# The second matrix of the last feed-forward network: seven block products in place of eight, in a half-pair order

## The chip, the cores and the metric

The kernel runs on one NeuronCore of a Trainium2 chip. The metric is the device time of one execution in microseconds (us). TensorE (PE) multiplies, VectorE (DVE) and ScalarE (ACT) do the elementwise work, GpSimd (POOL) does a little of it and issues some transfers, SyncE (SP) issues the loads of the weights. Each engine takes its instructions in the order in which they stand in its own queue.

## The reference, cut to what matters

A two-layer decoder trunk on 256 tokens of width 1024 in float32. Each layer is a mixer between two feed-forward networks; a last normalisation follows.

```python
def swiglu(h, w_in, w_out):            # w_in [1024, 5632], w_out [2816, 1024]
    gate, up = jnp.split(h @ w_in, 2, axis=-1)
    return (jax.nn.silu(gate) * up) @ w_out

for i in range(2):
    x = x + 0.5 * swiglu(rms_norm(x, ffn_norm[i, 0]), ffn_w_in[i, 0], ffn_w_out[i, 0])
    x = x + mixer(rms_norm(x, mix_norm[i]))     # 0: gMLP, 1: stick-breaking attention
    x = x + 0.5 * swiglu(rms_norm(x, ffn_norm[i, 1]), ffn_w_in[i, 1], ffn_w_out[i, 1])
return rms_norm(x, final_norm)
```

The change concerns the last `swiglu` (i = 1, second network) and the normalisation behind it.

## The kernel before, in words

Every matrix product is made of three TensorE products: each operand is split exactly into two float32r parts, `hi` (a cast on ACT) and `lo` (source minus hi, on DVE), and `mm3` adds lo·hi, hi·lo and hi·hi.

The weights are one stream of pieces of 128 x 1024 numbers (512 KB), in the order of use, kept by the class `Weights`. `run_to` (L66 to L88) issues a load on SP and, later, the split of a piece: an ACT cast (L81) and a DVE subtraction (L83). `get` asks for loads `RAW_AHEAD` = 7 and splits `SPLIT_AHEAD` = 5 pieces ahead of the piece in use; there are 7 buffers for raw pieces and 9 each for hi and lo.

A feed-forward network goes through 11 pairs of blocks ("pairs", 256 hidden features each). `ffn_in` multiplies the pair's gate and up columns (four pieces, 96 TensorE products of 256 columns) into two PSUM banks; DVE scales them by 1/rms (L449, L451), ACT applies silu (L450), DVE multiplies (L452), and the result is split (L153, L154). Two pairs later the pair's two pieces of the second matrix are multiplied. In the last network this is `out_add`: stationary the hidden block (128 features x 128 tokens), moving 512 columns of the weights, into four banks; 2 feature halves x 2 token halves x 2 column halves x 3 = 24 products of 512 columns for each pair, so eight block products for each pair.

At the start of the last network `norm.columns` and `norm.rows` (tag `pstf`) turn the sum of squares `acc`, which POOL adds up (L288), into 1/rms (`rT`, `diag`, `rb`). `back` transposes the residual stream and ACT copies it to `xo` (L812). Behind the last pair the output is finished in pieces of 512 and 256 columns: DVE adds (L854), ACT squares, DVE and ACT scale (L868, L870), SP stores (L873).

The order in an engine's queue is set by the framework's scheduler, which may take an instruction ahead of another that it deems late. `tc.keep_in_program_order` puts an instruction behind whatever was traced last for its engine. The stick-breaking attention ahead of the last network has its order written out by hand (`ATT_STEPS`).

Of the kernel before, what the change touches and what calls it, by code (L numbers as in the profile page):

```python
# [38 lines left out]
class Weights:  # L39
    """The weight matrices as a stream of [128, 1024] pieces in the order of use. Each is loaded  # L40
    once and split exactly into two float32r parts, w = hi + lo, some pieces ahead of its use."""

    def __init__(self, tc, raw_pool, hi_pool, lo_pool):
        self.nc = tc.nc
        self.keep_order = tc.keep_in_program_order
        self.strict = False
        self.behind = 0  # so many pieces keep their place
        self.piece = UNIT
        self.pools = raw_pool, hi_pool, lo_pool
        self.sources = []  # L50
        self.raw = {}
        self.parts = {}
        self.loaded = 0
        self.split = 0
# [36 lines left out]
    def get(self, i, inner):  # L91
        self.run_to(i + 1 + RAW_AHEAD, i + 1 + min(SPLIT_AHEAD, 2 + i // 2))
        hi, lo = self.parts.pop(i)
# [6 lines left out]
def trunk(  # L100
# [29 lines left out]
    hp = ctx.enter_context(tc.tile_pool(name="hp", bufs=4))  # L130
    scr = ctx.enter_context(tc.tile_pool(name="scr", bufs=8))
    small = ctx.enter_context(tc.tile_pool(name="small", bufs=3))
    pg = ctx.enter_context(tc.tile_pool(name="pg", bufs=4, space=PSUM))
    py = ctx.enter_context(tc.tile_pool(name="py", bufs=4, space=PSUM))

    def gbank(name):
        return pg.tile([P, 512], F32, tag="pg", name=name)

    def ybank(name):
        return py.tile([P, 512], F32, tag="py", name=name)  # L140

    def scratch(name, width=512):
        return scr.tile([P, width], F32, tag="scr", name=name, padded_shape=[P, 516])

    def mm3(o, a, b, first, last):
        """o (+)= a.T @ b for a, b each given as two float32r parts."""
# [9 lines left out]
    # The gMLP's blocks of 256 features: the u products, the mixing behind them, the products into  # L156
    # the residual stream behind that.
# [44 lines left out]
    plan11 = plan_ffn(1, 1)  # L202

# [39 lines left out]
    def warm_up(n):  # L243
        """Products of nothing, that wake the tensor engine's clock while the first loads run."""
# [24 lines left out]
    def prepare(d, gains, sq=True):  # L269
        """The parts of x*g of chunk d for the next products, and its share of the mean square."""  # L270
# [22 lines left out]
    def newton(o, root, v, w):  # L293
        """o = v**-0.5 from an estimate of v**0.5, with a step of Newton's; w is scratch."""
# [34 lines left out]
    def load_x(hf):  # L329
        """Half of x into the residual stream, its parts and its squares."""  # L330
# [33 lines left out]
    def bc2(ap):  # L364
        """[128, n] -> [128, 2, n], the same twice."""
# [6 lines left out]
    class Residual:  # L372
        """y.T = sum over chunks of W[chunk].T @ h[chunk], in four banks."""
# [50 lines left out]
    def project_rows(o, ids, xs, mid={}):  # L424
        """x.T W for a block of 256 features: [tokens, features] of two halves."""
# [17 lines left out]
    def ffn_in(tag, j, ids, mid={}, by_bank=False):  # L443
        """silu(gate) * up of 256 features, in two parts."""
# [16 lines left out]
    def ffn(tag, plan, gains, mid={}, by_bank=False, extra={}):  # L461
        """extra: what else is done ahead of a block's products into the residual stream."""
# [15 lines left out]
    # ======== layer 0: gMLP ========  # L478
# [17 lines left out]
    def spatial_weights(hf):  # L496
        """The causal W_s, transposed, and what the LayerNorm's shift and b_s add behind it:
        b_c * (row sum of W_s)[t] + b_s[t]."""
        gg = slice(hf * 4, hf * 4 + 4)
        nc.gpsimd.affine_select(  # L500
            ws3[:, gg],
            ws3[:, gg],
            pattern=[[0, 4], [-1, P]],
            compare_op=ALU.is_ge,
            fill=0.0,
            base=0,
            channel_multiplier=1,
# [394 lines left out]
```

## Time and profile before

| what | value |
|---|---|
| time, median of 3 runs | 1018.98 us (1018.62 to 1019.21) |
| profiled execution: its own time from first to last instruction (span) | 1016.9 us |
| TensorE busy | 998.7 us (98%), 8044 products |
| VectorE busy | 651.4 us (64%) |
| ScalarE busy | 499.6 us (49%) |
| GpSimd busy | 84.0 us (8%) |
| mean granted TensorE clock | 0.998 of full speed |
| DMA | 177 GB/s on the mean |

The profile gives no time for the profiled execution beyond its span; the median of the runs is 2.1 us above that span. Products of TensorE are pipelined, so one of them "takes" longer than the distance to the next; what counts is the distance between starts.

### The profile page before, as it was taken

Reading aid. Unit: us, or ns where it says so; the run is one execution under the profiler, and the core shown is the slowest. Engines: PE = TensorE matmul, PEld = TensorE weight load, DVE = VectorE, ACT = ScalarE, POOL = GpSimd, SP = SyncE. Lnnn points to the kernel's source line nnn. Section 1 sums busy time; section 2 is a strip of 40 time slices with the busy share of each in tenths; the row PEclk is TensorE's granted clock in tenths of the full one; section 3 lists DMA queues with packets and bytes.
Section 4 is the critical chain, followed back from the end, with each engine's and each line's share of the span. In section 5 each row is a group of like instructions: output and inputs, shape, how many; then the busy total and the mean of one; then the engine's idle time right before and its main releaser. Section 6 shows DMA issues by size and latency. Waiting matters only on the chain.

```text
span 1016.9 us, 19320 instructions
## 1 busy us (share of the span) xinstructions
PE 998.7 (98%) x8044; PEld 979.4 (96%) x8044; DVE 651.4 (64%) x852; ACT 499.6 (49%) x683; POOL 84.0 (8%) x122
## 2 busy tenths in 40 slices
PE   9999999999999999999999999999998899999997
PEld 8999999999999999999999999999998799999996
DVE  6865665676766774646569655564679975655553
ACT  7543434475544553434348444443476565444433
POOL 3000000010000300000003000000036420000002
PEclk9999999999999999999999999999999999999999
DMA  9965555656545365655564756555642436656511
GB/s 310 325 187 174 185 179 176 187 161 212 186 167 167 125 214 183 187 184 187 180 190 141 239 185 187 182 188 181 193 132 65 137 117 219 188 185 191 183 42 42
DMA packets 135208, 179.56 MB, mean 177 GB/s; under 512 B 5624, under 2 KB 119376, under 8 KB 135120
## 3 DMA queue, kind: packets, MB, share of 16 engines
q1 hardware_dynamic: 134768, 177.76, 54.9%
q8 instruction: 63, 1.03, 0.4%
q0 software_dynamic: 192, 0.52, 0.2%
q14 instruction: 25, 0.20, 0.1%
q10 hardware_dynamic: 160, 0.05, 0.0%
HBM read 176.73 MB, written 1.05 MB: 175 GB/s over the span
## 4 chain that ended last, share of the span: by engine, by line
PE 88%; DVE 6%; issue 2%; ACT 1%; DMA 1%; POOL 1%; SPq 0%; ACTq 0%; POOLq 0%; DVEq 0%
PE yo L148 2%; PE yo L150 2%; PE yo L149 2%; PE gb L148 2%; PE uc L149 2%; PE gc L148 2%; PE ub L149 2%; PE yb L148 2%; PE uc L150 2%; PE ub L150 2%; PE ub L148 2%; PE gb L150 2%; PE uc L148 2%; PE ud L150 2%; PE gc L150 2%
## 5 line engine op out<-in xcount | busy, mean ns | idle before, releaser
L81 ACT CAST whi<-raw 128x1024 fp32r<-128x1024 f32 (+1 forms) x333 | 342.3, 1044 | 403.3 <-issue 219.2
L83 DVE TENSOR_TENSOR wlo<-raw,whi 128x1024 fp32r<-128x1024 f32 (+1 forms) x333 | 400.9, 1221 | 203.2 <-ACT whi L81 202.4
L288 POOL TENSOR_TENSOR acc<-acc,sq 128x256 f32<-128x256 f32 x39 | 33.9, 870 | 566.9 <-ACT sq L287 564.9
L148 PE MATMUL ga<-xnh,wlo 128*128 128x256 f32 x176 | 50.7, 288 | 0.0
L148 PE MATMUL ya<-hha,wlo 128*128 128x256 f32 x176 | 50.0, 284 | 0.1
L148 PE MATMUL yc<-hhc,wlo 128*128 128x256 f32 x176 | 50.0, 284 | 0.1
L148 PE MATMUL yb<-hhb,wlo 128*128 128x256 f32 x176 | 50.0, 284 | 0.0
L148 PE MATMUL gd<-xnh,wlo 128*128 128x256 f32 x176 | 50.0, 284 | 0.0
L148 PE MATMUL gb<-xnh,wlo 128*128 128x256 f32 x176 | 49.9, 283 | 0.0
L148 PE MATMUL gc<-xnh,wlo 128*128 128x256 f32 x176 | 49.9, 283 | 0.0
L149 PE MATMUL ya<-hla,whi 128*128 128x256 f32 x176 | 49.8, 283 | 0.0
L149 PE MATMUL yb<-hlb,whi 128*128 128x256 f32 x176 | 49.8, 283 | 0.0
L149 PE MATMUL yc<-hlc,whi 128*128 128x256 f32 x176 | 49.7, 283 | 0.0
L150 PE MATMUL ud<-xnh,whi 128*128 128x256 f32 x176 | 49.7, 282 | 0.0
L150 PE MATMUL uc<-xnh,whi 128*128 128x256 f32 x176 | 49.6, 282 | 0.0
L149 PE MATMUL ub<-xnl,whi 128*128 128x256 f32 x176 | 49.6, 282 | 0.0
L149 PE MATMUL uc<-xnl,whi 128*128 128x256 f32 x176 | 49.6, 282 | 0.0
L150 PE MATMUL yb<-hhb,whi 128*128 128x256 f32 x176 | 49.6, 283 | 0.0
L148 PE MATMUL ua<-xnh,wlo 128*128 128x256 f32 x176 | 49.6, 282 | 0.0
L150 PE MATMUL ga<-xnh,whi 128*128 128x256 f32 x176 | 49.6, 282 | 0.0
L150 PE MATMUL ub<-xnh,whi 128*128 128x256 f32 x176 | 49.6, 282 | 0.0
L149 PE MATMUL gd<-xnl,whi 128*128 128x256 f32 x176 | 49.5, 281 | 0.0
(286 smaller groups left out, 3367.1 us busy)
## 6 DMA issues: line engine op xcount, KB each, us to landing
raw<-in_ffn_w_in_dram SPq DMA_DIRECT2D x176, 512.0 KB, 4.6
raw<-in_ffn_w_out_dram SPq DMA_DIRECT2D x88, 512.0 KB, 4.2
raw<-in_a_w_in_dram SPq DMA_DIRECT2D x32, 512.0 KB, 4.4
raw<-in_a_w_out_dram SPq DMA_DIRECT2D x16, 512.0 KB, 3.3
raw<-in_b_w_q_dram SPq DMA_DIRECT2D x8, 512.0 KB, 4.4
raw<-in_b_w_o_dram SPq DMA_DIRECT2D x8, 512.0 KB, 4.3
raw<-in_w_kv_dram SPq DMA_DIRECT2D x4, 512.0 KB, 4.2
xin<-in_x_dram SPq DMA_DIRECT2D x4, 256.0 KB, 4.5
```

The lines of the kernel that those rows point to most:

```text
L81: ins = nc.scalar.copy(hi[:, cc], raw[:, cc])
L83: ins = nc.vector.tensor_sub(lo[:, cc], raw[:, cc], hi[:, cc].bitcast(F32))
L148: nc.tensor.matmul(o, al, bh, start=first, stop=False, skip_group_check=True)
L149: nc.tensor.matmul(o, ah, bl, start=False, stop=False, skip_group_check=True)
L150: nc.tensor.matmul(o, ah, bh, start=False, stop=last, skip_group_check=True)
L288: nc.gpsimd.tensor_add(acc, acc, s)
```

## The change

In the last network the second matrix is multiplied by a scheme with seven block products for ten of the eleven pairs. For a pair, A is the hidden block as 2 x 2 blocks (token half by feature half) and B the 256 x 1024 weights as 2 x 2 blocks of 128 x 512. The eight products A·B become seven products of sums of blocks, each into a PSUM bank of its own (`q[1]` to `q[7]`) that is kept through all ten pairs; the four output blocks are put together from the seven banks at the end. The eleventh pair is multiplied plainly (`plain`).

What goes with it:

- The sums of A (`sums`: four DVE operations of 128 columns) are made in float32 from the hidden block, which is kept in the free halves of `xT`; then seven of the eight blocks are split (`parts`: an ACT cast and a DVE subtraction of 896 columns).
- The sums of B are made by accumulating transfers that POOL issues. `load` brings three blocks by SP; `first` splits these three (1536 columns) and issues one accumulating transfer of 512 KB; `second`, one half-pair later, splits two sums (1024 columns) and issues two accumulating transfers of 256 KB, the second of which reads what the first writes; `third`, a pair later, splits two more sums (1024 columns).
- The first matrix is multiplied by half pairs (`in_half`: gate and up of 128 features, 48 products) into one bank, `pi`, which has a single buffer from pair 2 on (the second halves of pairs 0 and 1 use another).
- From the last network's first normalisation on, all ACT, DVE, POOL and SP work is pinned to the order of the program; each pair's four pieces of the first matrix are split during the pair before (`weights`).
- For room in SBUF the whole kernel's stream has `RAW_AHEAD` 5, `SPLIT_AHEAD` 4, 5 raw buffers and 7 each for hi and lo.
- The final sums, squares and scalings are written anew for the seven banks (`finish`). One `affine_select` of the gMLP is pinned.

The core of the diff (comments are dropped in the new file):

```diff
-RAW_AHEAD = 7
-SPLIT_AHEAD = 5
+RAW_AHEAD = 5
+SPLIT_AHEAD = 4
...
-    rawp = ctx.enter_context(tc.tile_pool(name="rawp", bufs=7))
-    hip = ctx.enter_context(tc.tile_pool(name="hip", bufs=9))
-    lop = ctx.enter_context(tc.tile_pool(name="lop", bufs=9))
+    rawp = ctx.enter_context(tc.tile_pool(name="rawp", bufs=5))
+    hip = ctx.enter_context(tc.tile_pool(name="hip", bufs=7))
+    lop = ctx.enter_context(tc.tile_pool(name="lop", bufs=7))
...
+    psum.close()
+    pi = ctx.enter_context(tc.tile_pool(name="pi", bufs=1, space=PSUM))
+    pools["y"] = ctx.enter_context(tc.tile_pool(name="pq", bufs=7, space=PSUM))
...
+    pin = tc.keep_in_program_order
+
+    def pinned_split(h, l, src):
+        pin(nc.scalar.copy(h, src))
+        pin(nc.vector.tensor_sub(l, src, h.bitcast(F32)))
...
+        def load(self, j):
+            t = fm.tile([P, 3, 512], F32, tag="raw", bufs=3, name=f"fraw{j}")
+            for s, (m, n) in enumerate(((1, 1), (0, 0), (1, 0))):
+                pin(nc.sync.dma_start(t[:, s, :], self.block(j, m, n)))
...
+        def first(self, j):
+            p = self.parts[j] = {}
+            p["B22"], p["B11"], p["B21"] = self.split(j, 0, 0, 3)
+            pin(
+                nc.gpsimd.dma_start(
+                    self.raw[j][:, 0:2, :],
+                    self.block(j, 0, 1).unsqueeze(1).broadcast_to([P, 2, 512]),
+                    accum_op=ALU.add,
+                )
+            )
+
+        def second(self, j):
+            p = self.parts[j]
+            p["R3"], p["R1"] = self.split(j, 1, 0, 2)
+            t = self.raw[j]
+            pin(nc.gpsimd.dma_start(t[:, 1, :], self.block(j, 1, 1), accum_op=ALU.add))
+            pin(nc.gpsimd.dma_start(t[:, 2, :], t[:, 1, :], accum_op=ALU.add))
+
+        def third(self, j):
+            p = self.parts[j]
+            p["R2"], p["R4"] = self.split(j, 2, 1, 3)
...
+    PRODUCTS = {
+        1: ("A11", "B11"),
+        2: ("A12", "B21"),
+        3: ("S4", "B22"),
+        4: ("A22", "R4"),
+        5: ("S1", "R1"),
+        6: ("S2", "R2"),
+        7: ("S3", "R3"),
+    }
+    UNITS = NPAIR - 1
...
+    def weights(p):
+
+        W.run_to(first_id + p + 1 + RAW_AHEAD, first_id + p + 1)
...
+    def gate_up(j, m, bank):
+        gu = gus[j, m] = scratch(f"gud{j}_{m}")
+        pin(nc.vector.tensor_mul(pair(gu), pair(bank), bc2(rb)))
+        pin(nc.scalar.activation(gu[:, :T], gu[:, :T], AF.Silu))
+
+    def hidden(j, m):
+        f = fs[j] = xT[:, (j % 2) * 4 : (j % 2) * 4 + 4, :].rearrange("p a (b t) -> p (a b) t", b=2)
+        gu = gus.pop((j, m))
+        pin(nc.vector.tensor_mul(f[:, 2 * m : 2 * m + 2, :], pair(gu[:, :T]), pair(gu[:, T:])))
+
+    def sums(j):
+        f = fs[j]
+        pin(nc.vector.tensor_sub(f[:, 4, :], f[:, 2, :], f[:, 0, :]))
+        pin(nc.vector.tensor_sub(f[:, 6, :], f[:, 0, :], f[:, 1, :]))
+        pin(nc.vector.tensor_add(f[:, 5, :], f[:, 4, :], f[:, 1, :]))
+        pin(nc.vector.tensor_sub(f[:, 7, :], f[:, 3, :], f[:, 5, :]))
...
+    def rows():
+        norm.rows()
+        back()
+        W.strict = True
+
+    for j in range(NPAIR):
+        last = j == NPAIR - 1
         for m in range(2):
...
+            if m == 0 and j < UNITS:
+                forms.load(j)
+            in_half(j, m, bank, (norm.columns, rows) if (j, m) == (0, 0) else ())
+            if m == 0:
+                weights(4 * j + 4)
+                if j:
+                    parts(j - 1)
+                if j > 1:
+                    forms.third(j - 2)
+                weights(4 * j + 5)
+                gate_up(j, m, bank)
+                if 0 < j:
+                    forms.second(j - 1)
+                hidden(j, m)
+                if j == 2:
+                    q = {n: ybank(f"q{n}") for n in range(1, 8)}
+                if j > 1:
+                    out_add(j - 2, (1, 2, 3, 5))
+            else:
+                weights(4 * j + 6)
+                if not last:
+                    forms.first(j)
+                gate_up(j, m, bank)
+                weights(4 * j + 7)
+                hidden(j, m)
+                if not last:
+                    sums(j)
+                if j > 1:
+                    out_add(j - 2, (7, 6, 4))
+    parts(NPAIR - 1)
+    forms.third(UNITS - 1)
...
+    out_add(UNITS - 1, (1, 5, 7))
...
+    out_add(UNITS - 1, (6,))
...
+    out_add(UNITS - 1, (2, 3, 4))
...
+    plain(2, ("A11", "A12"), 0)
...
+    plain(3, ("A11", "A12"), 1)
...
+    plain(8, ("A21", "A22"), 1)
+    finish(1, 2)
...
+    for i in range(2):
+        cc = slice(i * 256, (i + 1) * 256)
+        plain(4, ("A21", "A22"), 0, cc)
+        add(xo[:, 0, cc], q[4][:, cc], 0.5, xo[:, 0, cc])
+        square(0, 1 + i, cc)
+    finish(0, 3)
```

## Rows read from the trace of the kernel before

**Rows 1.** Engines' busy time in two stretches: attention, and one pair.

```profile
757.00:805.00 48.00, 40.45 (x282) 36.11 (x282) 47.09 (x76) 31.76 (x65) 30.62 (x54) 1.00 0.38 119
...
863.50:880.30 16.80, 16.80 (x121) 15.82 (x120) 9.53 (x11) 7.11 (x9) 0.00 (x0) 1.00 0.59 186
```

**Rows 2.** Waits: engine and line, what it waited for, total, times, longest.

```profile
DVE gsd L449 <- PE gd L150: 30.2, 10, 10.8
```

**Rows 3.** TensorE in order of time at the borders of blocks of the last network.

```profile
846.38 0.48 PE L148 MATMUL yo<-whi,hld 128*128 128x512 f32 x1
...
981.23 0.40 PE L148 MATMUL yo<-whi,hld 128*128 128x512 f32 x1
...
986.72 0.28 PE L148 MATMUL gd<-xnh,wlo 128*128 128x256 f32 x1
...
998.08 0.40 PE L148 MATMUL yo<-whi,hld 128*128 128x512 f32 x1
...
1009.26 0.28 PE L150 MATMUL yo<-whi,hhd 128*128 128x256 f32 x1
```

**Rows 4.** Groups by line and shape in the last network: busy us, mean ns.

```profile
L83 DVE TENSOR_TENSOR wlo<-raw,whi 128x1024 fp32r<-128x1024 f32 x59 | 71.0, 1220 | 41.5 <-ACT whi L81 41.4
L81 ACT CAST whi<-raw 128x1024 fp32r<-128x1024 f32 x59 | 60.9, 1047 | 81.3 <-issue 45.0 <-PE gd L150 34.3 <-PE yo L150 1.7
...
L449 DVE TENSOR_TENSOR gsd<-gd,rb 128x512 f32<-128x512 f32 x11 | 7.6, 691 | 30.2 <-PE gd L150 30.2
...
L452 DVE TENSOR_TENSOR usd<-usd,gsd 128x512 f32<-128x512 f32 x11 | 7.5, 686 | 0.1
L450 ACT ACTIVATE gsd<-gsd 128x512 f32<-128x512 f32 x11 | 6.9, 628 | 12.8 <-DVE gsd L449 12.8
```

**Rows 5.** VectorE, then ScalarE, in order of time, where instructions follow without a wait.

```profile
897.81 1.21 DVE L83 TENSOR_TENSOR wlo<-raw,whi 128x1024 fp32r<-128x1024 f32 x1
898.94 0.68 DVE L452 TENSOR_TENSOR usd<-usd,gsd 128x512 f32<-128x512 f32 x1
899.54 1.21 DVE L83 TENSOR_TENSOR wlo<-raw,whi 128x1024 fp32r<-128x1024 f32 x1
...
897.49 0.63 ACT L450 ACTIVATE gsd<-gsd 128x512 f32<-128x512 f32 x1
898.02 1.04 ACT L81 CAST whi<-raw 128x1024 fp32r<-128x1024 f32 x1
```

**Rows 6.** From sum of squares to rb, four engines; then the copies to xo.

```profile
820.13 5.98 POOL L288 TENSOR_TENSOR acc<-acc,sq 128x256 f32<-128x256 f32 x7 [16.97 <-ACT sq L287]
...
826.81 0.50 PE L311 MATMUL pstf<-ones,acc 128*128 128x1 f32 x4
...
828.66 0.26 ACT L316 ACTIVATE rootf<-pstf,eps 128x2 f32<-128x2 f32 x1
...
828.95 0.16 DVE L317 TENSOR_SCALAR varf<-pstf 128x2 f32<-128x2 f32 x1 [3.44 <-ACT rootf L316]
...
829.81 0.48 DVE L320 TENSOR_SCALAR diag<-ident,rT 128x128 f32<-128x128 f32 x2
...
834.33 0.36 ACT L325 COPY rb<-pstf 128x256 f32<-128x256 f32 x1
...
845.73 2.02 ACT L812 COPY xo<-xb 128x512 f32<-128x512 f32 x4
```

**Rows 7.** Transfers: queue, count, KB each, median us from issue to landing.

```profile
raw<-in_ffn_w_out_dram SPq DMA_DIRECT2D x88, 512.0 KB, 4.2
...
out_dram<-xo SPq DMA_DIRECT2D x4, 256.0 KB, 2.0
...
kzh<-kzh POOLq DMA_DIRECT2D x2, 128.0 KB, 6.2
```

**Rows 8.** Behind the last product: VectorE, then ScalarE.

```profile
1009.77 0.42 DVE L854 SCALAR_TENSOR_TENSOR xo<-yo,xo 128x256 f32<-128x256 f32 x1
...
1012.57 0.91 ACT L870 ACTIVATE xo<-xo,fr 128x256 f32<-128x256 f32 x2 [0.93 <-DVE fr L298]
```

More of the change, by code (lines that the diff above doesn't have):

```diff
@@ L201, in trunk @@
     plan_o = [W.add(rows(b_w_o[0], P * b)) for b in range(8)]
-    plan11 = plan_ffn(1, 1)
+    plan11 = [
+        [[W.add(cols(ffn_w_in[1, 1], c0 + 256 * j, kh)) for c0 in (0, DFF)] for kh in range(2)] for j in range(NPAIR)
+    ]
+    plan_d = [W.add(rows(ffn_w_out[1, 1], 256 * (NPAIR - 1) + P * m)) for m in range(2)]
     xin = {}
@@ L499, in spatial_weights @@
         gg = slice(hf * 4, hf * 4 + 4)
[L500 to L507, printed above, removed]
+        tc.keep_in_program_order(
+            nc.gpsimd.affine_select(
+                ws3[:, gg],
+                ws3[:, gg],
+                pattern=[[0, 4], [-1, P]],
+                compare_op=ALU.is_ge,
+                fill=0.0,
+                base=0,
+                channel_multiplier=1,
+            )
         )
@@ new lines, in in_half @@
+    def in_half(j, m, bank, mid=()):
+        for kh in range(2):
+            if m == 0:
+                wd[kh] = [W.get_split(i, 256) for i in plan11[j][kh]]
+            for k4 in range(4):
+                k = kh * 4 + k4
+                for n, w in enumerate(wd[kh]):
+                    mm3(
+                        bank[:, n * T : (n + 1) * T],
+                        tuple(t[:, k4, m * P : (m + 1) * P] for t in w),
+                        (xnh[:, k, :], xnl[:, k, :]),
+                        k == 0 and n == 0,
+                        k == KC - 1,
+                    )
+            if kh < len(mid):
+                mid[kh]()
@@ L804, in back, with parts @@
+    def parts(j):
+        s0, s1 = (1, 8) if j < UNITS else (0, 4)
+        h = fm.tile([P, s1 - s0, P], F32R, tag="fsh", name=f"fsh{j}", padded_shape=[P, 7, P])
+        l = fm.tile([P, s1 - s0, P], F32R, tag="fsl", name=f"fsl{j}", padded_shape=[P, 7, P])
+        pinned_split(h, l, fs.pop(j)[:, s0:s1, :])
+        fparts[j] = {n: (h[:, s - s0, :], l[:, s - s0, :]) for n, s in SLOT.items() if s0 <= s < s1}
     def back():
@@ L811, in back @@
                     )
-                nc.scalar.copy(xo[:, tt, hf * 512 : (hf + 1) * 512], bank)
-    norm = Rms("f3")
-    hs = {0: ffn_in("d", 0, plan11["in", 0], {1: norm.columns, 2: norm.rows}), 1: ffn_in("d", 1, plan11["in", 1])}
-    back()
-    banks = [ybank(f"yo{i}") for i in range(4)]
-    def out_add(w, h, first, last, tts):
-        for tt in tts:
-            for hf in range(2):
-                mm3(
-                    banks[tt * 2 + hf],
-                    tuple(t[:, tt * P : (tt + 1) * P] for t in h),
-                    tuple(t[:, hf * 512 : (hf + 1) * 512] for t in w),
-                    first,
-                    last,
-                )
@@ new lines, in trunk, with at, add @@
+    parts(NPAIR - 1)
+    forms.third(UNITS - 1)
+    tail = [W.get_split(i, UNIT) for i in plan_d]
+    q[8] = pi.tile([P, 512], F32, tag="pi", name="q8")
+    gf = rawp.tile([P, D], F32, tag="raw", name="gf")
+    nc.sync.dma_start(gf, final_norm.unsqueeze(0).broadcast_to([P, D]))
+    def at(tt, n):
+        return xo[:, tt, n * 512 : (n + 1) * 512]
+    def add(o, a, scale, b, op=ALU.add):
+        nc.vector.scalar_tensor_tensor(o, a, scale, b, ALU.mult, op)
+    ss = {tt: small.tile([P, 4], F32, tag="ss", name=f"ss{tt}") for tt in range(2)}
@@ L864, in trunk @@
-        newton(r[:, 0:1], root, v[:, 2:3], r[:, 1:2])
-        for i, cc in enumerate(pieces):
-            o = xo[:, tt, cc]
-            if i == 1:
-                nc.vector.tensor_scalar_mul(o, o, r[:, 0:1])
-            else:
-                nc.scalar.mul(o, o, r[:, 0:1])
-        for hf in range(2):
-            cc = slice(hf * 512, (hf + 1) * 512)
-            nc.sync.dma_start(out[tt * P : (tt + 1) * P, cc], xo[:, tt, cc])
+        nc.vector.reduce_sum(v, ss[tt][:, :n], axis=mybir.AxisListType.X)
@@ new lines, in finish, with plain @@
+        nc.vector.tensor_scalar(v, v, 1.0 / D, RMS_EPS, ALU.mult, ALU.add)
+        nc.scalar.activation(root, v, AF.Sqrt)
+        newton(r[:, 0:1], root, v, r[:, 1:2])
+        nc.vector.tensor_scalar_mul(at(tt, 0), at(tt, 0), r[:, 0:1])
+        nc.scalar.mul(at(tt, 1), at(tt, 1), r[:, 0:1])
+        for h in range(2):
+            nc.sync.dma_start(out[tt * P : (tt + 1) * P, h * 512 : (h + 1) * 512], at(tt, h))
+    def plain(n, a, half, cc=slice(0, 512)):
+        for m in range(2):
+            c0 = half * 512
+            mm3(
+                q[n][:, cc],
+                fparts[NPAIR - 1][a[m]],
+                tuple(t[:, c0 + cc.start : c0 + cc.stop] for t in tail[m]),
+                n == 8 and m == 0,
+                m == 1,
+            )
```

117 lines of the change are left out of this document (77 added, 40 removed).

## The prediction

> **What bounds the kernel now.** I read the busy times first: TensorE is busy in practically all of a pair's 16.8 us, VectorE in 9.5 [rows 1]. Then the waits: VectorE's scaling of the gate waits for TensorE, 30 us in the last network, while TensorE waits for nobody there [rows 2]. So a product removed from TensorE is worth its full distance as long as the others keep up, and the reader should look at how much room they have.
>
> The order of TensorE's work gives the prices [rows 3]. From 981.23 to 986.72 stand 24 products of 512 columns, 0.229 us each; from there to 998.08 stand 96 of 256 columns, 11.36 us, with the change of block in it. A pair takes 16.85 us.
>
> **What is removed.** Ten pairs lose three products of 512 columns each: 10 x 3 x 0.229 = 6.9 us. A pair becomes 11.36 + 21 x 0.229 = 16.17 us, some 16.2 with the second change of block that the half-pair order brings.
>
> **What is added for VectorE and ScalarE.** From the groups, a VectorE operation of 1024 columns lasts 1.22 us and one of 512 lasts 0.69, an ACT cast of 1024 lasts 1.05 and a silu of 512 lasts 0.63 [rows 4]. Without a wait the next VectorE operation starts 1.13 us behind one of 1024 and 0.60 behind one of 512, and ACT's next 0.53 behind a silu of 512 [rows 5]. Scaled along these lines: 128 columns occupy VectorE 0.20 us, 256 0.33, 896 1.00, 1536 1.66; a silu of 256 holds ACT 0.32. A hop from engine to engine I put at 0.04 (828.66 + 0.26 to 828.95 is 0.03) [rows 6].
>
> All of this is pinned, so I follow the queue. Behind the gate of a second half VectorE needs: scaling 0.69, silu 0.32 (cast may follow), cast of a piece 1.05, hops 0.1, in all 2.15 us in which it has nothing else, since the subtraction of that piece stands next; then the subtraction 1.13, `hidden` 0.42, the four sums 0.96 (two wait for the one before), a subtraction 1.13, `parts` 1.00, `third` 1.13, a subtraction 1.13. That is 9.05 us from gate to gate. Behind the gate of a first half: 2.15 again, `second` 1.13, `hidden` 0.33, a subtraction 1.13, `first` 1.66, that is 6.40. Sum 15.45 us against TensorE's 16.2. In the steady state TensorE still sets the pace, with 0.75 us to spare; the single bank `pi` costs nothing there, because 12 and 9 products stand between two halves.
>
> **The start of the last network** has no such cover: pairs 0 and 1 have no products of the second matrix, 11.4 us of TensorE work each, against VectorE's loop. And the loop starts late. The sum of squares is complete at 820.13 + 5.98 = 826.11; column products 0.5, root 0.26, scale to `diag` 1.34 (828.95 to 830.29), row products about 0.5 as well, `rb` 0.36, with the hops 829.3 [rows 6]. Behind `rb` ACT's pinned queue holds the four copies to `xo`, 2.0 us in before [rows 6], which today come when nobody needs ACT; then the cast of piece 4. Subtractions of pieces 4 and 5, then: first gate of pair 0 at 834.8. I continue with the loop: without `second`, `first` waits for its own cast (1.47 us behind that of piece 6), so the second gate comes 5.2 us later, at 840.0; pair 1 at 847.9 (9.05 without `third`) and 854.3; pair 2 at 863.35. Only then is `pi` free, and the second half of pair 2 (5.68 us) ends at 869.75.
>
> TensorE alone would be there at 846.38 (today's start of the first second-matrix block, the same work behind it) + 5.68 + 12 x 0.229 + 5.68 = 860.5 [rows 3]. So 9.2 us are lost, first to pieces 7 and 11, which are split behind a gate and needed 2.8 us into the next half, then to the bank. Bounds: 0, if the queue were never late, and 11, if the transposes behind `xo` come late too. I take 9.2.
>
> **The accumulating transfers.** No row of before has one. The nearest are POOL's transfers of 128 KB in attention, 6.2 us to landing, four issued one behind another; SP's store of 256 KB lands in 2.0 us, its load of 512 KB in 4.2 [rows 7]. So one takes between 2.0 and 6.2; I take 4.3, near the load, since four sharing the engines make the 6.2 too long for one alone, and the store is not POOL's. The Trainium skill, DMA: Bandwidth & Descriptors, section on the anatomy of a SWDGE transfer, gives about 2.0 us plus the bytes at 436 GB/s, by estimate 2.6 us for 256 KB; the total by that figure would be 1020.4. The only rows of that queue here, 6.2 us for half the size, disagree with it.
>
> `second` issues two transfers, one waiting for the other, and `third` casts their result. In the steady state it asks for it 9.3 us after `second` has ended, so 2 x 4.3 = 8.6 is covered. At the end it is not. Pair 10's first gate is at 992.2 (983.15 + 9.05), `second(9)` ends at 995.6, the transfers at 1004.2, cast and subtraction at 1006.5. TensorE, from 869.75 with eight pairs of 16.2, ends its last half at 999.35, and 18 products of 512 columns later (1003.5) stands before product 6, which wants that operand: 3.0 us of waiting. The bounds are 0 (transfers of 2.0) and 7 (6.2).
>
> **The rest.** 512 KB by `first` has 8.8 us before it is asked for: nothing, unless it takes longer. A pair moves 2.75 MB of loads and 1 MB of accumulating transfers in place of 3 MB of loads; the transfer engines are 59% busy today [rows 1], so I take nothing for it, and if accumulating counts twice they would be close to full, which the late transfers below take in. Fewer buffers: loads still run five pieces ahead, some 14 us at 2.8 us for a piece, against 4.2 to landing [rows 7]: nothing. In attention VectorE is busy 47.1 of 48 us [rows 1]; one subtraction more that falls into that stretch, because splits run one piece less ahead, would cost up to 1.1 us; I take 0, as the same number of pieces is split in it. Behind the last product: it ends at 1009.54 today [rows 3], VectorE adds 0.23 us later because it is busy, and ACT scales two pieces in 0.91 [rows 8]; with one scaling of 512 columns (0.6), free engines, but two more tiny VectorE operations, I reckon 0.9 us less.
>
> **Sum.** From 1006.5: 30 products of 512 columns 6.87, 12 of 256 columns 1.42: last product ends at 1014.8, 5.3 later than today's 1009.54 (-6.9 + 9.2 + 3.0). With -0.9 behind it +4.4. The span would be 1021.3; the median of the runs stands 2.1 above the span, 1018.98 against 1016.9, so **1023.4 us**.
>
> **Rivals.** The other side: the queue keeps up at the start. If VectorE follows TensorE through pairs 0 to 2, the 9.2 us vanish: 1014.2. It decides at a loss of 4.8 us. For it: VectorE has 43% of its time free in a pair today, and transposes can fill a gap. Against: the pinned order leaves it idle twice in a pair, and the chain from the sum of squares cannot be shortened. 28%.
>
> The transfers are late in every pair. From the end of one `second` to that of the next the ring is two transfers, `third`'s cast 1.05, subtractions 2.26, scaling 0.69, silu 0.32, cast 1.05, subtraction 1.22, hops 0.2: 6.8 + 2L. From L = 4.7 that exceeds 16.2. At 5.0 it costs 0.6 us in each of eight pairs and more at the end, about 1030; at 6.2, 3.0 us in each, 24, and 4 to 5 at the end, about 1052. For it stands the 6.2 [rows 7]; against it that four shared the engines. 22%.
>
> Nothing measurable: transfers of 3 us (no wait at the end, 1020.4) with part of the start's loss gone. 14%.
>
> My forecast, start and end waiting but the pairs not: 36%.
>
> **How the numbers follow.** About 0.2% tells a change of this kernel from none, 1016.9 to 1021.0. Faster is the first rival, 0.28; same the third, 0.14; slower the forecast and the late transfers, 0.58. The range goes from 1013, which leaves out the first rival with its end wait gone as well, to 1042, which leaves out the worst transfers. The forecast's own range is 1021 to 1028.
>
> **What would show it.** TensorE's pairs 16.2 us apart in the middle (at 16.85 nothing was gained, at 19 the transfers are late); waits of TensorE for `wlo` in pair 1 and for the scaling in pair 2, some 9 us together before the first `third`; a wait for `third`'s result before the last product 6; `third` starting with or without a wait for a transfer. I am wrong if TensorE passes the end of pair 2 before 865, or if a POOL transfer of 256 KB takes over 4.7 us.

## The result and the profile after

The changed kernel takes 1027.07 us (median of 4 runs, 1026.06 to 1028.48) against 1018.91 of the kernel before (4 runs, 1018.62 to 1019.21): a ratio of 1.0081, 95% interval 1.0066 to 1.0095. It is slower, 3.7 us above the forecast of 1023.4 and just inside the forecast's own range of 1021 to 1028. The profiled execution has a span of 1026.1 us; before it was 1016.9.

The page of after begins with the busy times, share of the span and instructions of each engine:

```profile
PE 996.9 (97%) x8002; PEld 972.4 (95%) x8002; DVE 690.7 (67%) x918; ACT 519.0 (51%) x702; POOL 114.7 (11%) x151
```

Four stretches of it, cut where the prediction's terms end: from the last network's first product to the end of pair 2's second half, the eight pairs behind it, up to the end of the last product, and the rest. Columns: us, busy time and instructions of each engine, granted clock, share of the DMA engines, GB/s.

```profile
816.46:868.44 51.98, 47.22 (x347) 44.36 (x346) 36.47 (x53) 30.45 (x42) 10.64 (x12) 0.97 0.66 186
868.44:999.65 131.21, 127.73 (x922) 118.36 (x921) 98.22 (x126) 69.45 (x78) 23.92 (x24) 1.00 0.85 217
999.65:1017.46 17.81, 14.79 (x61) 11.26 (x59) 11.44 (x18) 5.89 (x12) 4.38 (x4) 0.90 0.11 19
1017.46:1026.10 8.64, 0.00 (x0) 0.00 (x0) 3.69 (x13) 3.27 (x9) 2.08 (x3) 0.68 0.32 121
```

The terms of the sum against these stretches (us; the predicted ones from the prediction's own times):

| stretch | predicted | measured | difference |
|---|---|---|---|
| first product of the last network, against 820.08 in before | 0 | -3.6 | -3.6 |
| to the end of pair 2 (820.08 to 869.75) | 49.7 | 52.0 | +2.3 |
| eight pairs of 16.2 | 129.6 | 131.2 | +1.6 |
| to the last product's end (999.35 to 1014.8) | 15.4 | 17.8 | +2.4 |
| behind it (today's 7.4 less 0.9) | 6.5 | 8.6 | +2.1 |

They add up to 4.8, which is what the span is above the predicted 1021.3. The forecast came this close by luck: an unforeseen gain of 3.6 us ahead of the change covered part of four costs of about 2 us each.

**Start.** A table load of ScalarE ahead of the root, which the prediction's chain had left out, then VectorE's scalings of the gate, in order of time (start, us):

```profile
823.23 1.28 ACT L324 ACT_TABLE_LOAD   x1 [1.83 <-PE pstf L319]
...
832.52 0.68 DVE L920 TENSOR_TENSOR gud<-i,rb 128x512 f32<-128x512 f32 x1
837.69 0.68 DVE L920 TENSOR_TENSOR gud<-i,rb 128x512 f32<-128x512 f32 x1
845.60 0.68 DVE L920 TENSOR_TENSOR gud<-i,rb 128x512 f32<-128x512 f32 x1
852.06 0.68 DVE L920 TENSOR_TENSOR gud<-i,rb 128x512 f32<-128x512 f32 x1
861.10 0.68 DVE L920 TENSOR_TENSOR gud<-i,rb 128x512 f32<-128x512 f32 x1
868.64 0.69 DVE L920 TENSOR_TENSOR gud<-i,rb 128x512 f32<-128x512 f32 x1 [0.75 <-PE i L155]
```

They are 5.17, 7.91, 6.46 and 9.04 us apart; predicted were 5.2, 7.9, 6.4 and 9.05. The gate behind them comes 7.5 us later and not 6.4, and it is the one that waits for TensorE, whose clock had fallen. TensorE had waited for `wlo` in pair 1 and in pair 2:

```profile
841.08 0.39 PE L153 MATMUL i<-xnh,wlo 128*128 128x256 f32 x1 [1.28 <-DVE wlo L83]
...
855.44 0.38 PE L153 MATMUL i<-xnh,wlo 128*128 128x256 f32 x1 [2.42 <-DVE wlo L83]
```

These are windows behind the second of these waits and at the end; the last column but two is the granted clock:

```profile
855.00:860.00 5.00, 4.56 (x24) 4.37 (x25) 4.93 (x10) 2.90 (x4) 0.31 (x1) 0.67 0.92 155
...
1005.00:1010.00 5.00, 4.57 (x12) 3.32 (x13) 3.97 (x6) 1.30 (x3) 0.00 (x0) 0.68 0.00 0
```

In the first window a product starts 2.8 us behind the one before it, in the second 2.1 us; soon behind each of these stops TensorE ran at the lower level of 1.2 GHz, for some 3.3 us of each window.

**Pairs.** What ScalarE waited for from 866 to 990 (us in total, times, longest), and the transfers of that stretch (queue, KB each, median us to landing):

```profile
ACT fh L819 <- DMA fraw<-in_ffn_w_out_dram: 5.3, 6, 1.8
ACT fh L819 <- DMA fraw<-fraw: 1.5, 2, 1.1
```

```profile
q1 hardware_dynamic: 16834, 20.35, 48.6%
q0 software_dynamic: 4337, 8.13, 40.5%
...
raw<-in_ffn_w_in_dram SPq DMA_DIRECT2D x25, 512.0 KB, 6.7
fraw<-in_ffn_w_out_dram SPq DMA_DIRECT2D x21, 256.0 KB, 7.5
fraw<-in_ffn_w_out_dram POOLq DMA_DIRECT2D x8, 512.0 KB, 8.1
fraw<-fraw POOLq DMA_DIRECT2D x8, 256.0 KB, 3.6
fraw<-in_ffn_w_out_dram POOLq DMA_DIRECT2D x7, 256.0 KB, 3.9
```

The 256 KB transfers take 3.6 to 3.9 us in the median, less than the 4.3 that I took; the two longest took 5.1 and 5.3, over the 4.7 that the prediction named as a sign of being wrong. What the casts wait for are mostly the results of `first`'s 512 KB (3.8 us; about 1 us of the first row is for SP's loads). The two queues hold the transfer engines for 89% of the time: 20.35 MB of loads for 48.6%, 8.13 MB of accumulating transfers for 40.5%, twice as much for a byte.

**End.** TensorE behind the last half, with two gaps (in brackets the idle time alone; the text counts from start to start):

```profile
1003.28 0.39 PE L155 MATMUL q<-fh,fsh 128*128 128x512 f32 x1
1005.37 0.73 PE L153 MATMUL q<-fh,fsl 128*128 128x512 f32 x2 [1.69 <-ACT fh L819]
...
1007.06 0.63 PE L155 MATMUL q<-fh,fsh 128*128 128x512 f32 x1
1007.48 0.63 PE L153 MATMUL q<-fh,fsl 128*128 128x512 f32 x1
...
1014.93 0.28 PE L155 MATMUL q<-whi,fsh 128*128 128x256 f32 x1
1016.47 0.39 PE L153 MATMUL q<-whi,fsl 128*128 128x256 f32 x1 [1.26 <-DVE fv L1030]
```

The first gap is the predicted wait for `third(9)`: 2.08 us from start to start, so 1.9 us beyond one product's distance of 0.23, in place of 3.0. Behind it products stand 0.43 us apart. The second gap, 1.54 us from start to start, I had not foreseen.

### The profile page after: what moved, and what is told of

It is laid out like the page before. It is cut to its first block, busy times and chain, and to the rows that moved or that the text cites. A ratio compares the mean times of both kernels' runs of the same rounds, so it can differ in the third digit from the quotient of the medians.

```text
span 1026.1 us, 19457 instructions
## 1 busy us (share of the span) xinstructions
PE 996.9 (97%) x8002; PEld 972.4 (95%) x8002; DVE 690.7 (67%) x918; ACT 519.0 (51%) x702; POOL 114.7 (11%) x151
## 5 line engine op out<-in xcount | busy, mean ns | idle before, releaser
L83 DVE TENSOR_TENSOR wlo<-raw,whi 128x1024 fp32r<-128x1024 f32 (+1 forms) x313 | 379.6, 1226 | 180.2 <-ACT whi L81 179.6
L153 PE MATMUL i<-xnh,wlo 128*128 128x256 f32 x352 | 100.8, 287 | 6.5 <-DVE wlo L83 3.7
L155 PE MATMUL i<-xnh,whi 128*128 128x256 f32 x352 | 99.4, 283 | 0.0
L154 PE MATMUL i<-xnl,whi 128*128 128x256 f32 x352 | 99.3, 282 | 0.0
L153 PEld LDWEIGHTS i<-xnh,wlo 128*128 128x128 f32 x352 | 66.6, 189 | 11.3 <-DVE gud L920 6.3
L154 PEld LDWEIGHTS i<-xnl,whi 128*128 128x128 f32 x352 | 66.9, 190 | 0.1
L155 PEld LDWEIGHTS i<-xnh,whi 128*128 128x128 f32 x352 | 66.9, 190 | 0.0
L820 DVE TENSOR_TENSOR fl<-fraw,fh 128x1024 fp32r<-128x1024 f32 (+1 forms) x30 | 42.0, 1400 | 23.3 <-ACT fh L819 23.3
L155 PE MATMUL ga<-xnh,whi 128*128 128x256 f32 x176 | 49.7, 282 | 0.0
L154 PE MATMUL gc<-xnl,whi 128*128 128x256 f32 x176 | 49.5, 281 | 0.0
L154 PE MATMUL gb<-xnl,whi 128*128 128x256 f32 x176 | 49.5, 281 | 0.0
```

Source lines behind the costliest of these rows:

```text
L83: ins = nc.vector.tensor_sub(lo[:, cc], raw[:, cc], hi[:, cc].bitcast(F32))
L153: nc.tensor.matmul(o, al, bh, start=first, stop=False, skip_group_check=True)
L154: nc.tensor.matmul(o, ah, bl, start=False, stop=False, skip_group_check=True)
L155: nc.tensor.matmul(o, ah, bh, start=False, stop=last, skip_group_check=True)
L820: pin(nc.vector.tensor_sub(l, src, h.bitcast(F32)))
```

## The experiments

Ratios are to the kernel before on the same chip, with their 95% intervals, 5 rounds each.

**1. The smaller stream alone.** The kernel before with

```diff
-RAW_AHEAD = 7
-SPLIT_AHEAD = 5
+RAW_AHEAD = 5
+SPLIT_AHEAD = 4
```

and the buffers and the pinned select of the change.

> The kernel before with the smaller stream alone: five raw buffers and seven of each split part in place of seven and nine, loads five and splits four pieces ahead, and the pinned GpSimd select; the last network is the old one. In the changed kernel the last network's first product starts 3.6 us earlier (816.46 against 820.08). Theory: this comes mostly from the two pieces whose split the pinned order moves out of the attention's tail into the start of the last network (two VectorE subtractions of 1.22 us and two casts), not from the buffers; here those two subtractions still stand in the attention, so the first product of the last network starts at 819 to 820 and the time is 1018 to 1019. Rival: the buffers do it, by keeping split work out of the attention altogether; then it starts near 816.5 and the time is about 1015.3.

1020.39 against 1020.06 us, ratio 1.0003 (0.9994 to 1.0011); the last network's first product starts at 821.96. Executions differ by more than 2 us in how they begin, so I count from the first product of the first network's second matrix (`ya`), which starts at 35.50 in before, 36.48 in after and 38.14 here: to the last network it is 784.6 us in before, 780.0 in after and 783.8 here. The buffers bring 0.8 us and not the whole gain. That the two splits do was still only argued, and fell in run 11.

**2. The start relieved.** The changed kernel with

```diff
+    def columns():
+        weights(4)
+        weights(5)
+        norm.columns()
...
                     forms.first(j)
+                if j == 0:
+                    copies()
                 gate_up(j, m, bank)
```

where `copies` holds the four ACT copies taken out of `back`.

> The changed kernel with two moves at the start of the last network: pieces 4 and 5 are split while VectorE and ScalarE wait for the sum of squares, and the four copies to xo stand behind the cast of the first pair's forms and not behind rb. Theory (the start's loss is the pinned queue of VectorE and ScalarE): the first gate starts near 827.4 in place of 832.5, the second near 833.3 in place of 837.7, the second half of pair 2 ends 4 to 5.5 us earlier than 868.4, and the time falls to 1021 to 1023.5. Rival (TensorE is held at the start by something else, loads or the bank alone): pair 2 ends within 1 us of 868.4 and the time stays at 1026 to 1028.

Ratio 1.0081 (1.0060 to 1.0103), no gain; yet the gates stand at 828.74 and 834.40, and pair 2 ends at 864.37, 4.1 us earlier (47.5 us behind the last network's first product and not 52.0). By the end of pair 10, at 999.48, all of it is lost: the eight pairs take 135.1 us. So the queue set the start, as predicted, and something in the pairs took the gain back.

**3. The wait at the end filled.**

```diff
+    for _ in range(9):
+        pin(nc.tensor.matmul(q[8], *filler, start=True, stop=True, skip_group_check=True))
     out_add(UNITS - 1, (6,))
```

> The changed kernel with nine products of 512 columns without use put into the free bank ahead of product 6 of the last unit, where TensorE waits 2.08 us for the result of the last transfers; the output is unchanged. The wait of TensorE is filled and not shortened. Theory: what the wait costs beyond its own length is the half clock behind it, 9 products 0.43 us apart in place of 0.227; with TensorE kept busy the granted clock stays full from 1000 to 1015 and the time falls by 1.5 to 2.2 us, to about 1025.2. Rival: the half clock comes by itself, for instance from all that ran before; then the half-clock stretch stands there as before and the time stays at 1027 or rises by up to 2 us.

Ratio 1.0100 (1.0087 to 1.0114), no gain in the time. In the stretch itself it went as the theory said: from the end of the last half to that of the last product 16.3 us (1002.18 to 1018.51) with nine products more, against 17.8, at full clock:

```profile
1005.00:1010.00 5.00, 4.24 (x19) 3.13 (x18) 2.41 (x3) 2.03 (x3) 0.00 (x0) 1.00 0.31 52
```

But the eight pairs, whose queues are those of the changed kernel, took 134.0 us in this execution, and hid it.

**4. TensorE's order held.** The first product of each group pinned, 12 behind first halves and 9 behind second ones.

```diff
+        if pinned:
+            tc.keep_in_program_order(ins)
+            pinned.clear()
```

> The changed kernel with TensorE's order in the last network held as it is written: 12 products of the second matrix behind each first half and 9 behind each second half, where it now has up to 15 to 17 behind first halves and 4 behind second ones. Theory: in the middle pairs the single bank pi then has 9 products, 2.04 us, of cover behind second halves, the waits for it (1.64, 0.48, 1.87 us) and the irregular pairs of 16.9 to 17.5 us go, every pair takes 16.1 to 16.2 us against 16.40 in the mean now, and the time falls by 1 to 2 us, to about 1025.3. Rival: VectorE's loop or the transfers set the pace in those pairs, not the bank; then pairs stay irregular with a mean of 16.3 to 16.5 and the time stays at 1027.

Ratio 1.0116 (1.0098 to 1.0135); the pairs took 137.3 us, 17.2 each. Of these 137.3 us, 3.7 are 16 products that stand ahead of the eight pairs in after, in the waits of pair 2; without them nothing is gained either. The theory falls: the bank's cover is not what made the pairs long. ScalarE's casts of the forms waited 9.9 us there for transfers of the second matrix (5.3 in after), and those of 512 KB took 9.7 us in the median (8.1).

**5. The changed kernel again.** No edit.

> The changed kernel itself once more, unchanged, beside the kernels that follow. So far its eight middle pairs took 131.2 us in one execution and 134.0 in another with the same queues up to there (the one with the filler products). Theory: the pairs are paced by transfers, whose durations differ from execution to execution, so the time scatters by some 3 us and lies 7 to 10 us above before; the kernel before scatters by less than 2 us. Rival: the changed kernel is as steady as before and the scatter came from the filler products; then all its times lie within 1.5 us.

Ratio 1.0094 (1.0080 to 1.0107), times 1027.65 to 1030.46 against 1019.35 to 1020.55 of before. It scatters more than before, and runs 2 to 4 differ from it by less than the intervals tell.

**6. No accumulating transfers.** The three `nc.gpsimd.dma_start(..., accum_op=ALU.add)` of `first` and `second` taken out, so the kernel leaves out the sums of B.

> The changed kernel without its accumulating transfers: the 30 sums of second-matrix blocks are left out (the splits take the blocks as they were loaded), all else stands. Theory: GpSimd's queue of three transfers a pair, slow because the transfer engines are 89% busy, sets the pace of the middle pairs, by the casts that wait for its results; without it every middle pair takes 16.0 to 16.2 us, the eight take 128.5 to 129.5 in place of 131 to 137, TensorE's wait of 2.1 us ahead of the last product 6 and the half clock behind it go, and the time is 5 to 8 us below the control. Rival: VectorE's pinned loop or the one bank sets the pace of the pairs; then they keep 16.4 to 16.9 us and only the end's 4 us are gained.

1020.20 us, ratio 1.0004 (0.9996 to 1.0013), 9.9 us below the control. The eight pairs:

```profile
869.40:996.13 126.73, 126.73 (x922) 118.46 (x921) 98.20 (x126) 68.39 (x78) 0.00 (x0) 1.00 0.49 158
```

TensorE never waits in them and the DMA engines are 49% busy. The accumulating transfers cost the pairs 4.5 us in the profiled execution of after (131.2), 4.7 in that of the control (131.5) and 7.3 in that of run 3 (134.0). The gain is larger than the theory's 5 to 8 us, which had the pairs at 16.0 or more; at the end the stretch to the last product takes 14.7 us in place of 17.8.

**7. No accumulating transfers, start relieved.** Edits 2 and 6 together.

> The kernel without the sums (left out as in the run before) with the earlier start: pieces 4 and 5 split ahead, the copies to xo later. With the sums in place the earlier start gained 4.1 us at the end of pair 2 and lost all of it by pair 10. Theory: it was lost because the transfers set the pace of the pairs; with them gone the 4 us stay, pair 2 ends near 864.4, and the time is 3.5 to 4.5 us below the kernel without sums, 1 to 3 us below before. Rival: the gain of the start is taken back by VectorE's loop all the same; then the time is within 1 us of the kernel without sums.

1016.46 us, ratio 0.9965 (0.9953 to 0.9978), 3.7 us below run 6. The gain of the start stays once the transfers are gone. This settles both: the start cost at least 3.7 us through VectorE's and ScalarE's queue, and what took its gain back were the transfers in the pairs.

**8. VectorE makes the sums.** The fourth block is loaded by SP (for room the scratch pool has four buffers in place of five), and four additions stand behind a second half's gate:

```diff
                 gate_up(j, m, bank)
+                if not last:
+                    forms.first_sums(j)
+                if 0 < j < UNITS:
+                    forms.second_sums(j - 1)
                 weights(4 * j + 7)
```

> The changed kernel with all sums kept but made by VectorE: the fourth block is loaded by SP like the others, and four additions of 512 columns a pair stand in VectorE's queue behind a second half's gate, where it waits 2.15 us for silu and cast. No accumulating transfers are left, at 3 MB of plain loads a pair as in before. Theory: the additions take 2.4 us, 0.25 more than the wait that hides them, so VectorE's loop is 15.8 to 15.9 us, still under TensorE's 16.1, and the time is within 1 us of the kernel without sums. Rival: VectorE becomes the bound, pairs take 16.4 to 17.5 us, and the time is that of the control or more.

Ratio 1.0113 (1.0097 to 1.0128): the rival. VectorE around one such gate:

```profile
920.34 0.69 DVE L927 TENSOR_TENSOR gud<-i,rb 128x512 f32<-128x512 f32 x1 [0.54 <-PE i L155]
920.95 0.68 DVE L860 TENSOR_TENSOR fraw<-fraw,b 128x512 f32<-128x512 f32 x1
921.66 0.69 DVE L861 TENSOR_TENSOR b<-b,fraw 128x512 f32<-128x512 f32 x1
922.27 0.68 DVE L873 TENSOR_TENSOR fraw<-fraw 128x512 f32<-128x512 f32 x1
922.99 0.69 DVE L874 TENSOR_TENSOR fraw<-fraw 128x512 f32<-128x512 f32 x1
923.60 1.22 DVE L83 TENSOR_TENSOR wlo<-raw,whi 128x1024 fp32r<-128x1024 f32 x1
...
930.54 0.69 DVE L927 TENSOR_TENSOR gud<-i,rb 128x512 f32<-128x512 f32 x1
```

The four take 2.65 us where the wait behind the gate is 1.42 (my 2.15 had counted the scaling itself), the next gate comes 10.2 us later and not 9.05, and the pair becomes 17.0 us.

**9. Two sums behind each gate.** The second step's sums, and the third split, behind the next first half's gate:

```diff
                 gate_up(j, m, bank)
+                if j > 1:
+                    forms.second_sums(j - 2)
...
                 hidden(j, m)
+                if j > 1:
+                    forms.third(j - 2)
```

> As the kernel with VectorE's sums, but with two additions behind each gate in place of four behind one: the two sums of the second step stand behind the next first half's gate, and the third split behind that gate too. Theory: four additions behind one gate failed because they take 2.65 us and the wait there, from the gate's end to the next subtraction, is only 1.42 us; two take 1.3 us and fit into each of the two waits (1.42 and 1.0 us), so VectorE's loop falls below TensorE's work, pairs take 15.9 to 16.2 us, and the time is within 1 us of the kernel without sums, that is 0 to 1.5 us above before. Rival: VectorE's additions cost their full time wherever they stand; then pairs take 16.6 to 17.1 us and the time is 7 to 12 us above before.

1018.50 us, ratio 0.9989 (0.9980 to 0.9998), with all sums in place: the eight pairs take 126.6 us. That is 1.1 us below before, where the theory had it 0 to 1.5 above; 1.3 us more than in run 6 are gained at the start, whose stretch to the end of pair 2 takes 50.4 us against 51.7. The edit also puts the third split of the last unit ahead of the last activations' split.

**10. With the start and the end.** Run 9 (with the third split of the last unit where it already stood there), the start of run 2, the addition of `q[4]` moved ahead, and

```diff
+        n = (1, 5)[i]
+        plain(n, ("A21", "A22"), 0, cc, True)
+        add(xo[:, 0, cc], q[n][:, cc], 0.5, xo[:, 0, cc])
...
+    pin(nc.scalar.activation(table, eps, AF.Sqrt))
```

> The kernel with two VectorE sums behind each gate, with the earlier start and three edits at the end: the last two pieces of the output get banks of their own (so that products of the second need not wait for the addition of the first), a square root without use loads ScalarE's table ahead of the squares, and the third split of the last unit stands ahead of the last activations' split. Theory: the start is worth 3.7 us, as without sums; at the end TensorE's wait of 1.5 us and 1.2 us of the table's load go, so the time is 5 to 7 us below the kernel before it in this list and 4 to 6 us below before. Rival: the end is bound by VectorE's and ScalarE's chain behind the last sums, not by these waits; then only the start's 3.7 us are gained.

1015.00 us, ratio 0.9959 (0.9945 to 0.9973), 3.5 us below run 9: only the start's part, the rival. Two windows of each, run 9 and then run 10, from the last half's end to the last product's, and behind it:

```profile
993.31:1008.05 14.74, 13.09 (x62) 10.36 (x60) 11.27 (x18) 5.72 (x12) 3.49 (x3) 1.00 0.00 1
1008.05:1016.60 8.55, 0.00 (x1) 0.00 (x0) 3.69 (x13) 3.35 (x9) 2.15 (x3) 0.61 0.33 123
```

```profile
989.54:1002.38 12.84, 12.84 (x62) 10.30 (x60) 10.44 (x15) 5.91 (x11) 2.16 (x2) 1.00 0.00 1
1002.38:1013.00 10.62, 0.00 (x1) 0.00 (x0) 6.00 (x18) 3.26 (x10) 3.45 (x4) 0.70 0.26 99
```

TensorE's gap is gone and 1.9 us with it, and the stretch behind it is 2.1 us longer: VectorE's adds queue up there, and its steps for the root fall beside GpSimd's products.

```profile
1004.27 0.16 DVE L303 RECIPROCAL fr<-fw 128x1 f32<-128x1 f32 x1 [0.22 <-ACT fw L1057]
1004.47 1.03 DVE L304 TENSOR_TENSOR fr<-fr 128x1 f32<-128x1 f32 x1
1005.54 0.65 DVE L305 SCALAR_TENSOR_TENSOR fr<-fr,fv 128x1 f32<-128x1 f32 x1
```

```profile
1004.23 2.63 POOL L1049 TENSOR_TENSOR xo<-xo,gf 128x512 f32<-128x512 f32 x3 [1.02 <-ACT junk L1048]
```

**11. Two splits out of the attention.** The kernel before with

```diff
     norm = Rms("f3")
+    W.strict = True
```

> The kernel before with one line: the splits of the pieces asked for at the start of the last network keep their place behind the attention's last preparation of x, so that two of them leave the attention (VectorE is busy 47.1 of 48 us there) and stand where VectorE waits for the sum of squares. Theory: this is what brought the changed kernel into the last network 3.6 us earlier, it has nothing to do with the seven products, and it is worth 2 to 4 us in the kernel before as well: 0.2 to 0.4% faster. Rival: the two splits only move the wait, to the first products of the last network that need them; then the time is that of before within 1 us.

1018.79 against 1019.59 us, ratio 0.9995 (0.9986 to 1.0003); the last network's first product starts at 821.27, 784.0 us behind the first `ya` product against 784.6 in before. That is 0.5 us, not 2 to 4: the theory falls.

**12. The place of h.** The kernel before with

```diff
-    hp = ctx.enter_context(tc.tile_pool(name="hp", bufs=4))
-    scr = ctx.enter_context(tc.tile_pool(name="scr", bufs=8))
     small = ctx.enter_context(tc.tile_pool(name="small", bufs=3))
+    scr = ctx.enter_context(tc.tile_pool(name="scr", bufs=8))
+    hp = ctx.enter_context(tc.tile_pool(name="hp", bufs=4))
```

> The kernel before with one edit of memory alone: the pools of hp and scr change places and stand behind the small one, as the diff has it, so that the h parts of the first networks lie at other addresses; every engine's queue is the same, instruction by instruction. In the kernels with the change the products of the second matrix in the networks ahead (yb, yc, queues unchanged) are in the mean 1.5% closer together than in before (280 against 283 ns each in the groups, 0.1178 against 0.1197 us from start to start), and TensorE comes to the attention 2.0 to 2.1 us earlier. Theory: the place of h makes that difference; here the yc products are 280 ns long, the attention starts 1.5 to 2.5 us earlier than in before, and the time falls by 0.15 to 0.25%. Rival: it is something else of the changed program; then the yc products stay at 283 ns and the time is that of before within 0.1%.

1016.68 against 1019.67 us, ratio 0.9972 (0.9962 to 0.9981). One group of the untouched network c, from 400 to 720 us, in before, after and this run (count, busy us, mean ns):

```profile
L150 PE MATMUL yc<-hhc,whi 128*128 128x256 f32 x144 | 40.7, 283 | 0.0
```

```profile
L155 PE MATMUL yc<-hhc,whi 128*128 128x256 f32 x144 | 40.3, 280 | 0.0
```

```profile
L150 PE MATMUL yc<-hhc,whi 128*128 128x256 f32 x144 | 40.3, 280 | 0.0
```

The products that read h (`ya`, `yb`, `yc`, `ys`) are the ones that became faster; those of `gc`, which do not read it, stay at 280 to 284 ns. The edit moves three pools, and what about the place of h matters was not found: by the order of the pools h lies elsewhere in run 1 too, and its products keep 283 ns.

The first product behind the attention's sum of squares starts at 746.58 in before, 744.52 in after and 744.25 here. Counted from the first `ya` product (35.50, 36.48 and 36.83) that is 711.1, 708.0 and 707.4 us, so the place of h brings after some 3.0 us ahead of the attention. From there to the last network it takes 73.50 us in before, 71.94 in after, 72.42 in run 1 and 73.56 here: most of these 1.6 us go with the smaller stream, by one execution each. Together they are 4.6 us; 3.6 were seen because after's execution began 1.0 us later than before's.

## Why the prediction was right, and where it was not

**The sign and the mechanism of the start** were right; that the time came within 3.7 us was luck. VectorE's pinned queue gave the gate distances to within 0.1 us, all but the last, TensorE waited for `wlo` in pairs 1 and 2 (1.6 and 2.8 us; in pair 2 not for the scaling, as I had it), and runs 2 and 7 show that moving work out of that queue gives 3.7 to 4.5 us back. TensorE's waits are 4.4 us and not some 9, because 17 products of 512 columns more than the program's order has there, 3.9 us, were done in pair 2. The term was 9.2; the stretch was 2.3 longer still. The first gate came 1.3 us later behind the first product than reckoned (16.06 against 14.72): the chain "column products 0.5, root 0.26" left out ScalarE's table load of 1.28 us between the two, which stands in before as well. The last gate came 1.1 us later than reckoned, and the clock had fallen behind TensorE's wait of 2.8 us.

**The pairs** were mis-sized. The step that failed is "512 KB by `first` has 8.8 us before it is asked for: nothing", together with "I take nothing for" the transfer engines: they were 85% busy in the pairs, and SP's loads of 512 KB landed in 6.7 us in place of 3.9 without the sums (run 6). I had followed only the two chained transfers and set the limit at 4.7 us for each; most took 3.6 to 3.9, and the pairs were late all the same. What I left out is the order of POOL's queue:

```profile
931.36 0.90 POOL L866 DMA_DIRECT2D fraw<-in_ffn_w_out_dram  x1 [9.35 <-DVE fl L820]
936.79 0.86 POOL L867 DMA_DIRECT2D fraw<-fraw  x1 [4.53 <-DMA fraw<-in_ffn_w_out_dram]
937.38 1.49 POOL L855 DMA_DIRECT2D fraw<-in_ffn_w_out_dram  x1
949.58 0.90 POOL L866 DMA_DIRECT2D fraw<-in_ffn_w_out_dram  x1 [10.70 <-DMA raw<-in_ffn_w_in_dram]
953.54 0.86 POOL L867 DMA_DIRECT2D fraw<-fraw  x1 [3.06 <-DMA fraw<-in_ffn_w_out_dram]
954.14 1.49 POOL L855 DMA_DIRECT2D fraw<-in_ffn_w_out_dram  x1
965.02 0.90 POOL L866 DMA_DIRECT2D fraw<-in_ffn_w_out_dram  x1 [9.39 <-DVE fl L820]
```

The next `first` (L855) stands behind L867, which waits until L866's data has landed; its 512 KB land 7 to 10 us later, the cast of `second` waits for them, and only then comes the next L866. In the first round shown, `first`'s split and the waiting cast were

```profile
932.77 1.76 DVE L820 TENSOR_TENSOR fl<-fraw,fh 128x1536 fp32r<-128x1536 f32 x1 [0.24 <-ACT fh L819]
...
946.97 1.05 ACT L819 CAST fh<-fraw 128x1024 fp32r<-128x1024 f32 x1 [1.84 <-DMA fraw<-in_ffn_w_out_dram]
```

The split ended at 934.53, L855 was issued at 937.38: 2.85 us in POOL's queue, more than the 1.84 that the cast waited. One round is 18.2 us from 931.36 and 15.4 from 949.58, where TensorE needs 15.8. So the second rival was at work, in four of the eight pairs (16.2 to 17.5 us, the others 15.8 to 15.9) and by another ring than the one that I priced. That the transfers did it is shown (run 6); how much of it is the order of the queue and how much the full transfer engines is not, since no run changed the order alone.

Unhindered, pairs take 15.84 us (run 6) and not 16.2, because 19 products of 512 columns stand in one and not 21: TensorE's order has moved 17 of them ahead into pair 2, where 29 stand and 12 were reckoned. So the 1.6 us of the table are 4.5 us of late transfers less 2.9 us of this.

Beside the rows: the Trainium skill, DMA: Bandwidth & Descriptors, section on the anatomy of a SWDGE transfer, by which 256 KB would take 2.6 us by estimate, does not agree with the 3.6 to 3.9 us here, for accumulating transfers on transfer engines 89% busy.

**The end.** The wait for `third(9)` was there, at 1.9 of the 3.0 us. Not in the sum were the half clock behind it, eight distances of 0.43 in place of 0.23 us, so 1.6 us (run 3 shows that it comes from the wait), and the 1.54 us at 1014.93, where the second piece in bank `q[4]` waits for VectorE's addition of the first. Run 10 gave the pieces banks of their own, and the gap was gone.

**Behind the last product** the step that failed is "one scaling of 512 columns (0.6), free engines", 0.9 us less. The engines are not free: 8.6 us in place of 6.5. VectorE's and ScalarE's steps for the other half of the tokens stand in the queues, and VectorE is slowed beside GpSimd (a step on one column 0.59 us in place of 0.16, a scaling of 512 columns 0.84 in place of 0.49). Taking TensorE's gap and the table load away did not shorten the whole (run 10). How the 2.1 us divide was not tried.

**In front** the step that failed is "Fewer buffers [...] nothing", by silence on addresses: the diff moves the h tiles, and their place is worth 3.0 us in the kernel before (run 12). "I take 0" for the attention failed too: it became 1.6 us shorter.

Seven products instead of eight are thus worth little here: 1015.0 us with sums by VectorE and a relieved start, against 1016.7 for the old scheme with h at the better place. By their ratios, 0.9959 and 0.9972, the intervals overlap.

## What to carry to other kernels

Price a queue of transfers as a loop of its own: each issue, each landing that the next one waits for, and what is queued behind it; and count the transfer engines' time by kind, since an accumulating byte took twice that of a load. When one engine is relieved by 4%, look first at the loops that lie within 4% of it; work for another engine goes into the waits that its trace shows, measured from the end of one instruction to the start of the next. And before a gain or loss ahead of a change is explained by its queues, look whether tiles have moved, and whether the two executions began alike.

## What the hardware showed that was not expected

- The place of a product's operand in SBUF changed its time: 283 or 280 ns in the mean for 256 columns, with the same instructions in the same order, and 0.28% of this kernel (run 12).
- Accumulating transfers held the transfer engines for 5.0% of the stretch for each MB, loads for 2.4%.
- Soon after products had started 2.1 and 2.8 us behind the ones before them, TensorE ran for some 3.3 us at half clock, long before the kernel's end in the second case; nine products without use in the first of these waits kept the clock up (1.00 in place of 0.68, run 3).
- VectorE's operations with two inputs lasted 0.65 and 1.03 us on one column beside a GpSimd product of two SBUF operands, and 0.16 otherwise; a reciprocal, with one input, lasted 0.16 beside the same product (run 10). The Trainium skill, SBUF — State Buffer, section "Who interferes with whom", says that a VectorE instruction with two inputs in SBUF contends with a GpSimd instruction that reads SBUF, because its second input comes through a read interface that the two share; these rows agree with it.
